# Cutting the last 128 rows into four pieces, and letting each late partial sum enter the result by its own matmul

## The chip, the cores and the metric

One core of a Trainium2 chip. The metric is the device time of one execution in microseconds, as the median of repeated runs. A profile's span, from the first to the last instruction, is some 1.7 us shorter than the time of the same run (667.04 against 668.75 in before). Engines: PE does matmuls, DVE and ACT sum rows, POOL issues the loads, SP the stores.

## The reference

```python
def setup_inputs():
    B, H, W = 4, 4224, 4224
    return {"x": np.random.randn(B, H, W).astype(np.float32)}

def reference(x):
    ps = np.cumsum(np.cumsum(x, axis=1), axis=2)
    diag = np.diagonal(ps, axis1=1, axis2=2)
    return np.cumsum(diag, axis=1).astype(np.float32)
```

All of x (285 MB in fp32) has to be read; what comes out is 4 x 4224 numbers.

## The kernel before

The loads cast to bf16 on the way (the page has 285.47 MB read from HBM, 142.47 MB on the queue). For most of x, matmuls with a selector matrix and row sums on DVE and ACT share the work. The last 384 outputs of the last batch are treated apart, as their rows arrive last: `part_a` is 256 rows, `part_b` the last 128, which come in three pieces of columns (`bcuts`). Each piece is divided among three engines (`shares`): its first `wp` columns go to PE, which folds them into 256 columns of PSUM; the next `wa` go to ACT; the rest to DVE.

```python
# ... after the loads of part_a:
            bcuts = [(2432, TB), (640, 2432), (0, 640)]
            for c0, c1 in bcuts:
                nc.gpsimd.dma_start(out=part_b[:, c0:c1], in_=x[b, TB:N, c0:c1])
# ... fold_a, carry, two scans and the store of the first 3840 outputs ...
        fold_b = psum_s.tile([P, 256], FP32, name="fold")
        fin_a = psum_s.tile([1, 2 * P], FP32, name="fin_a")
        fin_b = psum_s.tile([1, P], FP32, name="fin_b")
        shares = [(768, 512), (768, 512), (0, 320)]
        n = 1
        for i, ((c0, c1), (wp, wa)) in enumerate(zip(bcuts, shares)):
            fold_in(fold_b, part_b, c0, c0 + wp, 256, start=i == 0)          # PE
            act_sum(tsum[:, n : n + 1], part_b[:, c0 + wp : c0 + wp + wa])   # ACT
            if i == 2:
                row_sums(tsum[:, n + 2 : n + 3], fold_b)                     # DVE
            row_sums(tsum[:, n + 1 : n + 2], part_b[:, c0 + wp + wa : c1])   # DVE
            n += 2
            if i == 0:                                                       # PE, fp32
                matmul(fin_b, arows[:, 0:1], weights[:, 2 * P : GW], start=True)
                matmul(fin_b, arows[:, 1:2], weights[:, P : 2 * P])
                matmul(fin_a, arows[:, 0:1], weights[:, 0 : 2 * P], start=True)
                matmul(fin_a[:, P : 2 * P], arows[:, 1:2], weights[:, 0:P])
        ttot = last.tile([P, 1], FP32, name="ttot")
        row_sums(ttot, tsum)
        matmul(fin_b, ttot, weights[:, 0:P])
# ... yl = fin_a + c12, store; yl = fin_b + c12, store
```

`arows` are the row sums of part_a, `ttot` those of part_b. I call the four matmuls on arows "the fins" (the trace shows each fp32 matmul as two passes, so the two on fin_a are a group of x4), and "piece two" is the second of the pieces.

## Time and profile before

| | before |
|---|---|
| time, median of 3 runs (lowest to highest) | 669.03 us (668.8 to 669.93) |
| span of the profiled run | 667.04 us |
| DMA queue, share of 16 engines | 99.7% |
| DVE, PE, ACT busy | 50%, 32%, 21% |
| last landing (slowest engine's part of the last piece) | 663.43 us |
| yl<-fin_b, the last addition, starts | 664.77 us |

How to read it: the time is where the stream of loads ends, plus a tail. The tail has a part that never changes (from the start of yl<-fin_b to the end of the span 2.27 to 2.30 us in every one of the twenty profiles of this study: the addition, the store, the closing semaphores) and a part that the kernel decides. I call that part the **lag**: from the last landing to the start of yl<-fin_b, 1.34 us here. The lines are in the prediction.

### The profile page before, as it was taken

To read this page: it belongs to the slowest core of one execution; us is meant where nothing else is said; L and a number is where in the kernel's file an instruction comes from. 1 tells how busy PE (TensorE), PEld (TensorE's weight loads), DVE (VectorE), ACT (ScalarE), POOL (GpSimd) and SP (SyncE) were. 2 spreads that over 40 slices of the span, in tenths; PEclk is the share of its full clock that TensorE was granted. 3 is DMA by queue.
4 is the path that set the end of the run, shared out by engine and by line. 5 is a ranking of instruction groups with operands and counts; after the bars stand their busy time and mean duration, and the time that the engine had idled before them with its cause. 6 is when DMAs were issued, how large, how long until landed. Compare 5 with 4: busy or idle time off the path is not lost.

```text
span 667.0 us, 2828 instructions
## 1 busy us (share of the span) xinstructions
PE 215.1 (32%) x967; PEld 97.2 (15%) x967; DVE 336.3 (50%) x376; ACT 140.1 (21%) x225; POOL 27.0 (4%) x56
## 2 busy tenths in 40 slices
PE   0071522403118254140321633504032254250426
PEld 0030211101003022010110311201011122120202
DVE  2043617366924351745883415266398241635687
ACT  0001120406300103040630020304063002030436
POOL 5000000000000000000000000000000000001000
PEclk9995857666558586665655957567565586765758
DMA  9999999999999999999999999999999999999997
GB/s 203 219 219 219 218 219 219 217 217 216 208 215 219 219 219 217 216 219 219 219 219 215 216 211 217 220 219 216 216 216 219 220 215 218 216 215 219 216 207 144
DMA packets 7384, 143.25 MB, mean 215 GB/s; under 512 B 669, under 2 KB 842, under 8 KB 1866
## 3 DMA queue, kind: packets, MB, share of 16 engines
q0 software_dynamic: 7008, 142.47, 99.7%
q1 hardware_dynamic: 362, 0.61, 0.3%
q8 instruction: 7, 0.11, 0.1%
q14 instruction: 7, 0.06, 0.0%
HBM read 285.47 MB, written 0.07 MB: 428 GB/s over the span
## 4 chain that ended last, share of the span: by engine, by line
another core or an unknown queue 42%; DVE 25%; PE 23%; DMA 5%; issue 4%; DVEq 0%; POOLq 0%
PE d L198 23%; DVE acc L215 17%; DVE mu L218 7%; DMA strip<-in_x_dram 5%; PE fold L198 1%; DVE pu L215 0%; DVE c L397 0%; DVE c L218 0%; DVE tsum L215 0%; DVE acc L301 0%; DVE acc L304 0%; PE carry_ps L198 0%; DVE rows L331 0%; DVEq L218 0%
## 5 line engine op out<-in xcount | busy, mean ns | idle before, releaser
L218 DVE SCALAR_TENSOR_TENSOR mu<-strip,um 128x768 bf16<-128x768 bf16 (+1 forms) x129 | 110.7, 908 | 314.4 <-DMA strip<-in_x_dram 222.3
L198 PE MATMUL d<-strip,sel 128*11 128x384 bf16 x603 | 140.0, 406 | 344.4 <-DMA strip<-in_x_dram 344.4
L210 ACT ACTIVATE dump<-strip 128x416 bf16<-128x416 bf16 (+8 forms) x112 | 128.4, 1146 | 523.2 <-DMA strip<-in_x_dram 520.2
L215 DVE TENSOR_REDUCE acc<-strip 128x6 f32<-128x4608 bf16 (+6 forms) x23 | 195.9, 8518 | 0.0
L198 PEld LDWEIGHTS <-sel 128*11 128x11 bf16 x849 | 86.1, 101 | 526.3 <-issue 488.4
L198 PE MATMUL d<-mu,sel 128*11 128x384 bf16 x243 | 59.7, 355 | 67.5 <-DVE mu L218 67.4
L75 POOL DMA_DIRECT2D strip<-in_x_dram x24 | 16.5, 687 | 555.5 <-DVE acc L215 414.5
L210 ACT ACTIVATION_READ_ACCUMULATOR dump<-strip 128x1 f32 x112 | 20.9, 186 | 0.0
L218 DVE DVE_READ_ACCUMULATOR mu<-strip,um 128x1 f32 x129 | 10.6, 82 | 0.0
L198 PE MATMUL d<-ident,rows 128*11 128x128 f32 x24 | 5.2, 378 | 16.5 <-DVE rows L340 16.5
L198 PE MATMUL fold<-strip,ident_h 128*128 128x480 bf16 (+1 forms) x14 | 4.3, 458 | 8.4 <-DMA strip<-in_x_dram 8.4
L198 PE MATMUL d<-halves,rows 128*11 128x64 f32 x48 | 5.7, 304 | 0.0
L198 PEld LDWEIGHTS d<-halves,rows 128*11 128x11 f32 x48 | 5.1, 136 | 2.1 <-issue 2.1
L198 PEld LDWEIGHTS d<-ident,rows 128*11 128x11 f32 x24 | 2.6, 118 | 18.2 <-DVE rows L340 11.5
L215 DVE TENSOR_REDUCE pu<-d 11x1 f32<-11x384 f32 x4 | 2.2, 546 | 5.5 <-PE d L198 5.5
L397 DVE TENSOR_TENSOR_SCAN c<-ones_row,carry,c 11x384 f32<-11x384 f32 x4 | 4.0, 1006 | 0.1
L397 DVE TENSOR_TENSOR_SCAN c<-ones_row,carry,d 11x384 f32<-11x384 f32 x4 | 4.0, 1001 | 0.1
L198 PEld LDWEIGHTS <-ident_h 128*128 128x128 bf16 x20 | 2.2, 112 | 12.2 <-issue 11.8
L215 DVE TENSOR_REDUCE parts<-strip 128x3 f32<-128x3072 bf16 x1 | 3.4, 3350 | 0.0
L198 PE MATMUL d<-hmu,sel 128*11 128x384 bf16 (+2 forms) x3 | 0.7, 286 | 6.7 <-DVE hmu L218 6.7
L372 POOL DMA_DIRECT2D strip<-in_x_dram x2 | 1.4, 716 | 29.2 <-DVE acc L215 29.2
L215 DVE TENSOR_REDUCE tsum<-strip 128x1 f32<-128x384 bf16 (+2 forms) x3 | 1.7, 568 | 0.9 <-DMA strip<-in_x_dram 0.9
(78 smaller groups left out, 36.0 us busy)
## 6 DMA issues: line engine op xcount, KB each, us to landing
strip<-in_x_dram POOLq DMA_DIRECT2D x19, 6336.0 KB, 69.6
strip<-in_x_dram POOLq DMA_DIRECT2D x5, 3168.0 KB, 55.3
strip<-in_x_dram POOLq DMA_DIRECT2D x1, 1080.0 KB, 45.3
strip<-in_x_dram POOLq DMA_DIRECT2D x1, 768.0 KB, 48.2
head<-in_x_dram SPq DMA_DIRECT2D x1, 528.0 KB, 3.9
strip<-in_x_dram POOLq DMA_DIRECT2D x1, 448.0 KB, 51.1
strip<-in_x_dram POOLq DMA_DIRECT2D x1, 416.0 KB, 49.5
strip<-in_x_dram POOLq DMA_DIRECT2D x1, 160.0 KB, 51.4
```

The lines of the kernel that those rows point to most:

```text
L75: nc.gpsimd.dma_start(out=o, in_=x[b, r0 : r0 + f * P, :].rearrange("(p f) w -> p f w", f=f))
L198: nc.tensor.matmul(o, lhsT=lhsT, rhs=rhs, start=start, stop=False, skip_group_check=True)
L210: nc.scalar.activation(out=dump[:, :w], in_=src, func=ACT.Copy, accum_out=acc)
L215: nc.vector.reduce_sum(out=acc, in_=src, axis=AX.X)
L218: nc.vector.scalar_tensor_tensor(out=o, in0=i, scalar=1.0, in1=m, op0=ALU.mult, op1=ALU.mult, accum_out=acc,)
L372: nc.gpsimd.dma_start(out=part_a[:, :, c0:c1], in_=src_a[:, :, c0:c1])
L397: nc.vector.tensor_tensor_scan(out=c12[:, i, :], data0=ones_row, data1=src, initial=carry[:, i : i + 1], op0=ALU.mult, op1=ALU.add,)
```

## The change

The intent: make the piece that arrives last small, so that little is left to sum when it lands, and spare the reduction `ttot` at the very end: sums that come late enter fin_b by a matmul of their own. The fold narrows to 128 columns, and yl<-fin_a with its store moves forward.

```diff
-            bcuts = [(2432, TB), (640, 2432), (0, 640)]
+            bcuts = [(2688, TB), (1024, 2688), (384, 1024), (0, 384)]
...
-        shares = [(768, 512), (768, 512), (0, 320)]
+        shares = [(640, 384), (640, 512), (0, 320), (0, 128)]
         for i, ((c0, c1), (wp, wa)) in enumerate(zip(bcuts, shares)):
+            if i < 2:
+                fold_in(fold_b, part_b, c0, c0 + wp, P, start=i == 0)
+                a, v = tsum[:, 2 * i + 1 : 2 * i + 2], tsum[:, 2 * i + 2 : 2 * i + 3]
+            else:
+                a, v = ttot[:, 2 * i - 3 : 2 * i - 2], ttot[:, 2 * i - 2 : 2 * i - 1]
+            act_sum(a, part_b[:, c0 + wp : c0 + wp + wa])
+            row_sums(v, part_b[:, c0 + wp + wa : c1])
             if i == 0:
+                # fin_a's two matmuls, then fin_b's two, on arows
+                nc.vector.tensor_add(
+                    out=yl[:, : 2 * P], in0=fin_a, in1=c12[0:1, 1, : 2 * P]
+                )
+            if i == 1:
+                row_sums(tsum[:, 5:6], fold_b)
+                row_sums(ttot[:, 0:1], tsum[:, 0:6])
+                matmul(fin_b, ttot[:, 0:1], weights[:, 0:P])
-        row_sums(ttot, tsum)
-        matmul(fin_b, ttot, weights[:, 0:P])
+        for k in range(1, 5):
+            matmul(fin_b, ttot[:, k : k + 1], weights[:, 0:P])
...
```

More of the change, by code (lines that the diff above doesn't have):

```diff
@@ L421 @@
         row_sums(arows, asum)
-        fold_b = psum_s.tile([P, 256], FP32, name="fold")
+        fold_b = psum_s.tile([P, P], FP32, name="fold")
         fin_a = psum_s.tile([1, 2 * P], FP32, name="fin_a")
         fin_b = psum_s.tile([1, P], FP32, name="fin_b")
-        shares = [(768, 512), (768, 512), (0, 320)]
-        n = 1
+        yl = last.tile([1, GW], FP32, name="yl")
+        ttot = last.tile([P, 5], FP32, name="ttot")
+        shares = [(640, 384), (640, 512), (0, 320), (0, 128)]
         for i, ((c0, c1), (wp, wa)) in enumerate(zip(bcuts, shares)):
-            fold_in(fold_b, part_b, c0, c0 + wp, 256, start=i == 0)
-            act_sum(tsum[:, n : n + 1], part_b[:, c0 + wp : c0 + wp + wa])
-            if i == 2:
-                row_sums(tsum[:, n + 2 : n + 3], fold_b)
-            row_sums(tsum[:, n + 1 : n + 2], part_b[:, c0 + wp + wa : c1])
-            n += 2
+            if i < 2:
[5 more added lines that the diff above has]
+            row_sums(v, part_b[:, c0 + wp + wa : c1])
@@ L436 @@
             if i == 0:
+                matmul(fin_a, arows[:, 0:1], weights[:, 0 : 2 * P], start=True)
+                matmul(fin_a[:, P : 2 * P], arows[:, 1:2], weights[:, 0:P])
                 matmul(fin_b, arows[:, 0:1], weights[:, 2 * P : GW], start=True)
                 matmul(fin_b, arows[:, 1:2], weights[:, P : 2 * P])
-                matmul(fin_a, arows[:, 0:1], weights[:, 0 : 2 * P], start=True)
-                matmul(fin_a[:, P : 2 * P], arows[:, 1:2], weights[:, 0:P])
-        ttot = last.tile([P, 1], FP32, name="ttot")
@@ L442 @@
-        row_sums(ttot, tsum)
-        matmul(fin_b, ttot, weights[:, 0:P])
-        yl = last.tile([1, GW], FP32, name="yl")
-        for fin, c0, c1 in ((fin_a, 0, 2 * P), (fin_b, 2 * P, GW)):
-            nc.vector.tensor_add(
-                out=yl[:, c0:c1], in0=fin, in1=c12[0:1, 1, c0:c1]
-            )
-            nc.sync.dma_start(
-                out=out[b, T0 + c0 : T0 + c1].unsqueeze(0), in_=yl[:, c0:c1]
-            )
+                nc.vector.tensor_add(
+                    out=yl[:, : 2 * P], in0=fin_a, in1=c12[0:1, 1, : 2 * P]
+                )
@@ new lines @@
+            if i == 1:
[4 more added lines that the diff above has]
+            matmul(fin_b, ttot[:, k : k + 1], weights[:, 0:P])
+        nc.sync.dma_start(
+            out=out[b, T0 : T0 + 2 * P].unsqueeze(0), in_=yl[:, : 2 * P]
+        )
+        nc.vector.tensor_add(
+            out=yl[:, 2 * P :], in0=fin_b, in1=c12[0:1, 1, 2 * P :]
+        )
@@ L455 @@
+        nc.sync.dma_start(out=out[b, T0 + 2 * P : N].unsqueeze(0), in_=yl[:, 2 * P :])
 _INS = ['x']
```

## The prediction

> **What bounds the kernel now.** I read the page top down: engine shares, the 40 slices, then the chain that ended last, and after that the timeline of the last ten microseconds engine by engine. The 40 slices say what sets nearly all of the time:
>
> ```profile
> DMA  9999999999999999999999999999999999999997
> GB/s 203 219 219 219 218 219 219 217 217 216 208 215 219 219 219 217 216 219 219 219 219 215 216 211 217 220 219 216 216 216 219 220 215 218 216 215 219 216 207 144
> ```
>
> Every slice but the last has the DMA engines at 90% or more, and the page's queue section puts 99.7% of 16 engines' span on the software queue, while the busiest compute engine, DVE, is at 50%. The kernel is one stream of loads of about 663 us plus a tail after the last byte. The change moves no byte in or out of that stream: bcuts still cover the same 4096 columns of the last 128 rows. So only the tail can move.
>
> The tail is read from DVE's timeline, because the last stretch of the chain alternates between DVE and PE:
>
> ```profile
> 660.30 0.66 DVE L215 TENSOR_REDUCE asum<-fold_a 128x2 f32<-128x512 f32 x1
> 661.06 0.16 DVE L215 TENSOR_REDUCE arows<-asum 128x2 f32<-128x10 f32 x1
> 661.14 0.54 DVE L215 TENSOR_REDUCE tsum<-strip 128x1 f32<-128x384 bf16 x1
> 662.62 0.69 DVE L215 TENSOR_REDUCE tsum<-strip 128x1 f32<-128x512 bf16 x1 [0.94 <-DMA strip<-in_x_dram]
> 663.22 0.41 DVE L215 TENSOR_REDUCE tsum<-fold 128x1 f32<-128x256 f32 x1
> 663.55 0.47 DVE L215 TENSOR_REDUCE tsum<-strip 128x1 f32<-128x320 bf16 x1
> 664.13 0.16 DVE L215 TENSOR_REDUCE ttot<-tsum 128x1 f32<-128x8 f32 x1
> 664.21 0.40 DVE L446 TENSOR_TENSOR yl<-fin_a,c 1x256 f32<-1x256 f32 x1
> 664.77 0.28 DVE L446 TENSOR_TENSOR yl<-fin_b,c 1x128 f32<-1x128 f32 x1 [0.16 <-PE fin_b L198]
> ```
>
> ```profile
> 661.37 0.60 PE L198 MATMUL fin_b<-weights,arows 128*1 128x128 f32 x4 [0.39 <-DVE arows L215]
> 661.80 0.81 PE L198 MATMUL fin_a<-weights,arows 128*1 128x256 f32 x4
> 662.64 0.49 PE L198 MATMUL fold<-strip,ident_h 128*128 128x256 bf16 x3
> 664.35 0.38 PE L198 MATMUL fin_b<-weights,ttot 128*1 128x128 f32 x2 [1.22 <-DVE ttot L215]
> ```
>
> To be seen: DVE has one real wait, 0.94 us for the second piece of the last rows; from 662.62 it runs without a gap until ttot. The landings in the trace (last of a load's semaphore counts) are 660.44, 662.60 and 663.43 us for the three pieces. ACT's sum of the third piece starts at 663.51 and its accumulator read ends at 664.08; DVE's ends at 664.02. So after the last byte (663.43) come: sum 0.65 us, ttot at 664.13 (0.16), one matmul in two passes at 664.35 (0.38), yl at 664.77 (0.28), the output's issue at 665.07, its landing at 666.13, closing semaphores until 667.04. Some 3.6 us in all, of which the change can touch the first 1.3 us: 0.2% of the time.
>
> [...] In the trace DVE does run in program order: yl<-fin_a, ready since the 662.62 at which fin_a ended, stands until 664.21 behind everything written before it. [...] 320, 384 and 512 columns take 474, 543 and 686 ns, 1.1 ns per column. [...] The trace: the 16 counts of the last piece come from 661.24 to 663.43. [...]
>
> **The change, part by part.**
>
> Landings. On the slowest of the 16 engines a row of 1280 bytes took 97 ns from start to start, one of 3584 bytes some 265: proportional to bytes plus about 3 ns. Pieces of 1408, 1664, 640 and 384 columns are 8 rows each on that engine. Scaling the old landings, they come at about 660.14, 662.13, 662.91 and 663.47. The last byte is 0.04 us later (8 more rows at 3 ns, one more semaphore write). The one more load costs POOL 0.55 us near 612, 50 us before its data, hidden.
>
> What it removes from the end: the wait of ttot for both sums. ACT's part of the last piece falls from 320 to 128 columns: 0.47 to 0.31 us (0.83 ns per column, from 512 and 320), DVE's from 320 to 256: 0.47 to 0.41. The reduction ttot (0.16 and some 0.1 for its wait) leaves the end. The fold of piece two halves: 414 to 281 ns (estimate, 1.04 ns per column less).
>
> What it adds: four matmuls of two passes, each pass 0.108 us after the last (the four fin_b passes of before start at that spacing), so 0.22 us each.
>
> What it moves, and this decides: the order of instructions on DVE is now: first piece's sum, yl<-fin_a, second piece's sum, fold, ttot, third piece's sum, fourth's, yl<-fin_b. Worked through, with starts 0.08 us or so ahead of the previous end where nothing is waited for:
> - arows is where it was, 661.06 to 661.22, as nothing ahead of it depends on the new cuts. PE starts fin_a (now first) at 661.37: starts at 0, 0.215, 0.43, 0.54, last end 662.18. fin_b's passes follow until PE is free at 662.45[...].
> - DVE: yl<-fin_a can't start before 662.22 (0.04 after PE, as at 664.77 before) and holds DVE for 0.33. Piece two has been there since 662.13, so it now waits behind yl: start 662.55 in place of 662.17.
> - sum of 512 columns holds 0.60: fold at 663.15, ends 663.43; ttot with a wait of 0.10 at 663.53; third piece's sum at 663.61, ends 664.08; fourth's at 664.01, ends 664.42.
> - ACT: second piece done at 662.92, third at 663.57, fourth at 664.07: never last.
> - PE: total's matmul at 663.74, ACT's of piece three behind it; DVE's of piece three at 664.13; then ACT's of piece four at 664.35; DVE's of piece four could start at 664.47 but PE is free at 664.56: two passes, end 664.94.
> - yl<-fin_b at 664.98, against 664.77 before: 0.2 us later. The output's issue, landing and closing follow at the same distance; the first output leaves two microseconds earlier, which nothing waits for.
>
> Sum: gains of 0.06 to 0.16 (smaller sums) and 0.26 (ttot), taken back because DVE is not free when the last piece lands (664.01 against 663.47). Net +0.2 us: 669.03 + 0.2 = 669.2.
>
> **Rivals.** (1) The intended one: the end hangs on the last landing. Then from 663.47: 0.08 start, 0.41 sum, 0.06, two matmuls 0.60, yl at about 664.66, 0.1 us faster: 668.9. For it: DVE did wait 0.94 us for piece two before, so there is slack in its queue; against it: fin_a on PE ends at 662.18, after piece two has landed, so yl<-fin_a uses up that slack. (2) The stream decides: the extra piece, smaller rows, or another spread of the 16 engines move the last landing. For it: the engines finish 2.2 us apart, so one slow engine is what counts, and the three runs of before lie 1.1 us apart with nothing changed. Against: bytes per engine are the same[...]. 0 to +0.3 us beyond mine, or noise of either sign. (3) PE becomes the bound because its granted clock drops to half in the tail: the passes would double and add some 0.5 us, 669.7. Before, it was full from 658 to past 665, and the change adds PE work; unlikely.
>
> **Range and chances.** All three rivals lie within 0.7 us, 0.1% of the time. The spread of runs (668.8 to 669.93) is wider than the effect, so the range is mostly that spread: 668.6 to 669.9. A change of 2% would be 13 us, more than everything after the last byte; 0.01 for each side is left for the unforeseen, 0.98 for within 2%.
>
> **What would show it right or wrong.** Right: in DVE's timeline yl<-fin_a runs for about 0.4 us at 662.2 and the second piece's sum begins directly after it, not with a wait for a DMA; there is no wait between it and the last piece's sum, which begins 0.5 us after its landing; ttot's last matmul waits for DVE or PE, not ACT; yl<-fin_b stands later after the last landing than the 1.34 us of before (mine: 1.5). Wrong: a DMA wait ahead of the last sum on DVE, yl<-fin_b within 1.25 us of the last landing (rival 1), or a last landing more than 0.2 us from its old place (rival 2).

Piece two's five folds: their spacing was not measured in before, where folds of 256 columns start 108 ns apart. The sum has DVE reach the fold at 663.15, behind piece two's sum, and took the folds as done by then, the author's estimate; it comes to yl<-fin_b at 664.98, 0.2 us later than before, and so to 669.2. The 1.04 ns per column in the estimate for the fold is the slope of DVE's long sums in before: 5.55 us for 5184 columns, 11.35 for 10752.

## The result, and the profile after

| | before | after |
|---|---|---|
| time, median of 6 runs (lowest to highest) | 669.29 (668.8 to 669.93) | 669.97 (668.85 to 670.82) |
| span of the profiled run | 667.04 | 667.99 |
| last landing | 663.43 | 663.38 |
| start of yl<-fin_b | 664.77 | 665.70 |
| lag | 1.34 | 2.32 |

All kernels gave correct results. The ratio is 1.001, interval 0.9997 to 1.0022. The predicted 669.2 missed by 0.8 us, and 669.97 lies above the stated 668.6 to 669.9. The profiled run itself took 669.70 us.

The stream is much what it was (of the page's DMA digits only the last differs; the GB/s differ by 8 at most in a slice before the last):

```profile
DMA  9999999999999999999999999999999999999996
GB/s 202 219 219 219 218 219 217 219 219 219 216 211 214 214 220 219 219 219 217 214 219 218 219 219 219 216 212 216 216 219 219 218 215 214 219 218 219 219 204 132
```

The timeline of DVE in the changed kernel (start, duration, engine, line, operation, what it waited for):

```profile
660.57 0.16 DVE L215 TENSOR_REDUCE arows<-asum 128x2 f32<-128x10 f32 x1
...
662.35 0.41 DVE L443 TENSOR_TENSOR yl<-fin_a,c 1x256 f32<-1x256 f32 x1 [1.16 <-PE fin_a L198]
662.69 0.66 DVE L215 TENSOR_REDUCE tsum<-strip 128x1 f32<-128x512 bf16 x1
663.80 0.29 DVE L215 TENSOR_REDUCE tsum<-fold 128x1 f32<-128x128 f32 x1 [0.44 <-PE fold L198]
...
665.70 0.28 DVE L455 TENSOR_TENSOR yl<-fin_b,c 1x128 f32<-1x128 f32 x1 [0.63 <-PE fin_b L198]
```

And PE's:

```profile
660.88 1.44 PE L198 MATMUL fin_a<-weights,arows 128*1 128x256 f32 x4
662.11 1.06 PE L198 MATMUL fin_b<-weights,arows 128*1 128x128 f32 x4
663.10 0.66 PE L198 MATMUL fold<-strip,ident_h 128*128 128x128 bf16 x5
664.41 1.25 PE L198 MATMUL fin_b<-weights,ttot 128*1 128x128 f32 x10 [0.65 <-DVE ttot L215]
```

The order is the predicted one (yl<-fin_a, then piece two's sum directly behind it). What is not predicted: the fins take 2.29 us where 1.25 was reckoned, so piece two's folds end at 663.76 and not before the 663.15 at which the sum has DVE reach them, and DVE waits. The durations double as PE's granted clock halves (1.00 to 0.50; a pass takes 0.213 us in place of 0.108). The view by stretches shows it; its columns are the stretch, its length, busy us of PE, PEld, DVE, ACT and POOL with instruction counts, then the granted clock (the share of its full clock that PE was given), the DMA share and GB/s. First the kernel before, then the changed one:

```profile
657.00:660.50 3.50, 1.48 (x10) 0.56 (x9) 3.01 (x7) 2.27 (x6) 0.00 (x0) 1.00 1.07 211
660.50:663.50 3.00, 2.21 (x14) 1.08 (x13) 1.96 (x5) 1.44 (x4) 0.00 (x0) 1.00 0.45 83
```

```profile
657.00:660.50 3.50, 1.44 (x12) 0.94 (x12) 2.97 (x6) 2.31 (x7) 0.00 (x0) 0.95 1.09 212
660.50:663.50 3.00, 2.89 (x16) 1.28 (x14) 1.63 (x4) 1.77 (x6) 0.00 (x0) 0.50 0.53 90
```

Granted clock 1.00 against 0.50 from 660.5 to 663.5. The trace's clock records give the edges: before, full from 655.60 to 665.84 (10.24 us); after, full from 653.34 to 660.16 (6.82 us), half to 663.58 (3.42 us), full again.

### The profile page after: what moved, and what is told of

It reads as the page before. It is cut to its first block, busy times and chain, and to the rows that moved or that the text cites. A ratio compares the mean times of both kernels' runs of the same rounds, so it can differ in the third digit from the quotient of the medians.

```text
span 668.0 us, 2857 instructions
## 1 busy us (share of the span) xinstructions
PE 214.5 (32%) x979; PEld 97.8 (15%) x979; DVE 336.6 (50%) x377; ACT 140.4 (21%) x227; POOL 27.5 (4%) x57
## 4 chain that ended last, share of the span: by engine, by line
another core or an unknown queue 38%; DVE 24%; PE 22%; DMA 12%; issue 4%; DVEq 0%; POOL 0%; POOLq 0%
PE d L198 21%; DVE acc L215 16%; DMA strip<-in_x_dram 12%; DVE mu L218 6%; PE fin_b L198 0%; DVE pu L215 0%; DVE c L218 0%; PE fin_a L198 0%; PE fold L198 0%; DVE acc L304 0%; DVE acc L301 0%; PE fold_a L198 0%; POOL strip L372 0%; PE carry_ps L198 0%
## 5 line engine op out<-in xcount | busy, mean ns | idle before, releaser
L210 ACT ACTIVATE dump<-strip 128x416 bf16<-128x416 bf16 (+9 forms) x113 | 128.6, 1138 | 522.7 <-DMA strip<-in_x_dram 519.9
L198 PE MATMUL d<-mu,sel 128*11 128x384 bf16 x243 | 58.3, 346 | 67.5 <-DVE mu L218 67.3
L75 POOL DMA_DIRECT2D strip<-in_x_dram x24 | 16.5, 688 | 556.0 <-DVE acc L215 416.9
L198 PE MATMUL fold<-strip,ident_h 128*128 128x128 bf16 (+1 forms) x18 | 4.7, 432 | 9.2 <-DMA strip<-in_x_dram 9.2
L372 POOL DMA_DIRECT2D strip<-in_x_dram x2 | 1.4, 714 | 27.6 <-DVE acc L215 27.6
L375 POOL DMA_DIRECT2D strip<-in_x_dram x4 | 2.2, 550 | 7.9 <-DMA strip<-in_x_dram 7.9
```

The source lines that it names most:

```text
L75: nc.gpsimd.dma_start(out=o, in_=x[b, r0 : r0 + f * P, :].rearrange("(p f) w -> p f w", f=f))
L198: nc.tensor.matmul(o, lhsT=lhsT, rhs=rhs, start=start, stop=False, skip_group_check=True)
L210: nc.scalar.activation(out=dump[:, :w], in_=src, func=ACT.Copy, accum_out=acc)
L372: nc.gpsimd.dma_start(out=part_a[:, :, c0:c1], in_=src_a[:, :, c0:c1])
```

## The experiments

**Theory (clock):** the difference in lag is the clock's, which depends on when the clock happens to turn in a run, not on the change. **Rivals:** (order) the new order on DVE costs it, at any clock; (joins) the five matmuls at the end cost it.

One table for all profiles; the times are medians of the runs with that kernel. "On" is when the clock turned full at the end of the stream, "tail" the granted clock from 660.5 to 663.5, "lead" the time from the start of arows to the last landing.

| run | on | tail | lead | last landing | lag | time (runs) |
|---|---|---|---|---|---|---|
| before | 655.60 | full | 2.37 | 663.43 | 1.34 | 669.29 (6) |
| before_again | 653.67 | half | 2.79 | 663.53 | 2.27 | 669.79 (1) |
| after | 653.34 | half | 2.81 | 663.38 | 2.32 | 669.97 (6) |
| after_again | 652.92 | full | 2.81 | 663.75 | 1.26 | 669.00 (5) |
| after_third | 656.25 | full | 2.41 | 664.13 | 1.55 | 669.77 (6) |
| before_warm | 652.54 | full | 2.65 | 663.44 | 1.34 | 670.26 (5) |
| before_warm_b | 652.70 | full | 2.64 | 663.49 | 1.34 | 669.37 (6) |
| before_warm2 | 653.33 | full | 2.78 | 664.49 | 1.34 | 669.82 (6) |
| after_warm | 654.17 | full | 2.67 | 663.75 | 1.30 | 668.83 (5) |
| after_warm_b | 657.06 | full | 2.26 | 664.96 | 1.70 | 670.45 (6) |
| after_warm2 | 655.57 | full | 2.39 | 664.79 | 1.58 | 670.48 (6) |
| cuts_only | 653.60 | half | 2.81 | 663.41 | 2.22 | 670.26 (5) |
| joins_only | 652.79 | full | 2.78 | 663.49 | 1.39 | 669.43 (6) |
| yl_late | 653.86 | half | 2.81 | 663.65 | 2.37 | 670.02 (1) |
| after_fins2 | 653.87 | half | 2.80 | 663.63 | 3.61 | 671.54 (1) |
| no_fold2 | 653.57 | half | 2.84 | 663.58 | 1.43 | 668.99 (5) |
| no_fold2_b | 653.31 | half | 2.80 | 663.56 | 1.43 | 669.46 (5) |
| no_fold2_warm | 655.39 | full | 2.41 | 663.56 | 1.42 | 668.88 (5) |
| seven_joins | 654.94 | full | 2.81 | 663.65 | 1.42 | 669.11 (5) |
| seven_joins_warm | 653.80 | full | 2.68 | 663.44 | 1.43 | 669.12 (5) |

### Both kernels once more: after_again, before_again, after_third

No edit.

> The changed kernel once more, unaltered. Theory (clock): in the first profile the granted clock was 0.5 from 660.2 to 663.6 us, so the ten matmul passes ahead of piece two's folds took twice as long, the fold came to DVE at 663.80 in place of my 663.15, and yl<-fin_b stood 2.32 us after the last landing. [...]this profile either shows the clock full through 660 to 664 and yl<-fin_b at about 1.5 to 1.6 us after the last landing, or half there and again 2.2 to 2.4. Ratio over five rounds 1.0005 to 1.0015. Rival (order on DVE alone): 2.2 to 2.4 whatever the clock.

> The kernel before once more, unaltered, for a second sample of the clock's phase. Clock theory: full clock from 660 to 664 again gives yl<-fin_b 1.3 to 1.4 us after the last landing; half clock there gives 1.9 to 2.5, since ten passes stand ahead of the second fold here too. Rival (the old order is immune): 1.3 to 1.4 whatever the clock.

> The changed kernel unaltered, for another profile and five more times. Lag 1.25 to 1.6 us if the clock is full from 660 to 664, 2.2 to 2.4 if half; span less 2.27 us less the lag is the last landing, which in the profiles so far lay anywhere from 663.4 to 664.8. Ratio to before within 0.0015 of 1, with either sign.

Ratios: after_again 0.9998 (0.9985 to 1.001), so the expected 1.0005 to 1.0015 was missed; after_third 1.0009 (0.9993 to 1.0025). The kernel before, at half clock; DVE, PE, and the stretch:

```profile
662.72 0.69 DVE L215 TENSOR_REDUCE tsum<-strip 128x1 f32<-128x512 bf16 x1 [1.36 <-DMA strip<-in_x_dram]
664.24 0.42 DVE L215 TENSOR_REDUCE tsum<-fold 128x1 f32<-128x256 f32 x1 [0.84 <-PE fold L198]
...
665.80 0.28 DVE L446 TENSOR_TENSOR yl<-fin_b,c 1x128 f32<-1x128 f32 x1 [0.15 <-PE fin_b L198]
```

```profile
663.54 0.67 PE L198 MATMUL fold<-strip,ident_h 128*128 128x256 bf16 x3
```

```profile
660.50:663.50 3.00, 2.92 (x11) 1.10 (x10) 1.44 (x4) 1.48 (x5) 0.00 (x0) 0.50 0.46 85
```

The old kernel has the same wait for PE's fold (0.84 us) and loses 0.93 us of lag (2.27 against 1.34): the clock hits it as it hits the changed one, and the changed kernel at full clock has 1.26. So the 1 us between the first two profiles is not the change's. That shows only that lag and clock go together; the interventions below test the direction.

after_third has full clock but a late turn-on (656.25) and an arows that is late against the stream (lead 2.41), as in the very first profile of before. This is the case the prediction was worked out for:

```profile
661.72 0.16 DVE L215 TENSOR_REDUCE arows<-asum 128x2 f32<-128x10 f32 x1
...
662.87 0.41 DVE L443 TENSOR_TENSOR yl<-fin_a,c 1x256 f32<-1x256 f32 x1 [0.53 <-PE fin_a L198]
663.21 0.66 DVE L215 TENSOR_REDUCE tsum<-strip 128x1 f32<-128x512 bf16 x1
663.81 0.27 DVE L215 TENSOR_REDUCE tsum<-fold 128x1 f32<-128x128 f32 x1
...
665.68 0.28 DVE L455 TENSOR_TENSOR yl<-fin_b,c 1x128 f32<-1x128 f32 x1 [0.62 <-PE fin_b L198]
```

From the start of arows: yl<-fin_a after 1.15 (predicted 1.16), piece two's sum 1.49 (1.49), fold 2.09 (2.09), yl<-fin_b 3.97 (3.92). Piece two landed at 662.79, and its sum stands behind yl<-fin_a until 663.21. Lag 1.55, predicted 1.51.

### Holding the clock full: before_warm, after_warm, and again as _b

The edit, in both kernels; dummy matmuls into a bank nobody reads, in places where PE waits (three ahead of the carry, one behind it, three behind the second fold_a):

```diff
+            def keep_warm(n):
+                for _ in range(n):
+                    matmul(warm, ident_h, wide_of[0][:, :512], start=True)
...
+            keep_warm(3)
         carry_ps = psum_s.tile([NG, 2], FP32, name="carry_ps")
...
+            keep_warm(1)
         carry = smalls.tile([NG, 2], FP32, name="carry")
...
         fold_in(fold_a, part_a, c0, cp, 256)
+        keep_warm(3)
```

> The kernel before with the same seven dummy matmuls. Clock theory: lag of yl<-fin_b 1.3 to 1.4 us, time at the lower end of before's runs, 668.5 to 669.0, and 0.1 to 0.3 us under after_warm: with the clock equal, my +0.2 for the change is left. Rival (only the changed kernel is touched by the clock): no gain over before, ratio 1.000 within 0.0005.

> The changed kernel with seven dummy matmuls of 512 columns in PE's idle time of the last rows (three before the carry, one after it, three after the second fold_a), so that [...]the clock stays full. Clock theory: no 0.5 between 657 and 664, folds of piece two done by 663.1, yl<-fin_b 1.45 to 1.65 us after the last landing, 668.9 to 669.4 us, 0.5 to 0.9 faster than the changed kernel of the same rounds. Rival (DVE's order or the five last matmuls cost the time): lag stays at 2.2 or more, and the time with the changed kernel's.

> The kernel before with the seven dummies, again. Clock theory: this profile has full clock from 660 to 664 and lag 1.3 to 1.4; slow runs, if any, are late streams. If the profile falls on half clock in the tail in spite of the dummies, they don't hold it, and after_warm's five fast runs were luck.

> The changed kernel with the seven dummies, again. Clock theory: full clock in the tail, lag 1.25 to 1.6, span between 667.0 and 668.7 by where the stream ends. Luck: a run at half clock with lag 2.2 or more.

Ratios to before: before_warm 1.0006 (0.9992 to 1.002), after_warm 0.9989 (0.9977 to 1.0002), before_warm_b 0.9998 (0.9984 to 1.0013), after_warm_b 1.0009 (0.9994 to 1.0024). All four profiles have full clock in the tail, and lags of 1.30 to 1.70 only. With the dummies of the later runs it is eight of eight, against five of twelve without. The sharpest pairs have nearly the same turn-on: without dummies, all seven runs in which the clock turned on between 653.31 and 653.87 fell back to half at 660; with them, before_warm2 (653.33) and seven_joins_warm (653.80) did not.

The times are another matter, and here the expectation failed: before_warm had three of five runs at 670.3 to 670.5, and after_warm_b five of six above 670. The one profile among those, after_warm_b, has full clock and a lag of 1.70, but its **stream** ended at 664.96, 1.5 us later than in the first profile. Its third load landed at 97.6 us against 95.3 in before, long ahead of the first dummy, so the dummies didn't cause that delay. The same holds for all four late streams (after_third, before_warm2, after_warm_b, after_warm2): the 25th load, which landed at 649.58 in before, was already 0.67, 1.07, 1.55 and 1.39 us late, and no dummy runs before 655. The stream's end is a second draw, made before the tail begins. What the unprofiled slow runs of before_warm had, I can't say.

### More dummies: before_warm2, after_warm2

Ten in place of seven, two of them ahead of the last matmuls of d.

> The kernel before with ten dummy matmuls of 512 columns: two ahead of the last part of d, two before the carry, two after it, four after the second fold_a. [...] Clock theory: all five runs in the fast group (under 669.2), none near 670. In the first try with seven dummies three of five were at 670.3 and I saw no profile of those; if the five split again, the dummies do something else than keep the clock, and this theory needs another support. Rival (two groups from something other than the clock): about half of the runs at 669.6 to 670.1.

> The changed kernel with the same ten dummies. Clock theory: all five runs under 669.2, mean within 0.2 us of before_warm2; the changed kernel's slower average is then its slow group alone. Rival (the change costs time at any clock): 0.2 to 0.5 us over before_warm2.

Ratios 1.0002 (0.999 to 1.0013) and 1.0011 (0.9999 to 1.0024). Both profiles: full clock, lag 1.34 and 1.58, but streams that ended at 664.49 and 664.79. The expected "all under 669.2" failed for the times. As a test of the time it is inconclusive; as a test of the clock it adds two profiles at full clock. before_warm2 is useful otherwise: its stream is 1.06 us later than before's, and the lag is the same 1.34.

### One half of the change at a time: cuts_only, joins_only

cuts_only has the new pieces and shares with the old joining; joins_only the old pieces with the new joining:

```diff
 # cuts_only, against the changed kernel
-            if i < 2: ... else: ...    (own columns of ttot, own matmuls)
+            if i == 1:
+                row_sums(tsum[:, n : n + 1], fold_b)
+                n += 1
+        row_sums(ttot, tsum)
+        matmul(fin_b, ttot, weights[:, 0:P])
 # joins_only, against the changed kernel
+            bcuts = [(2432, TB), (640, 2432), (0, 640)]
+        shares = [(768, 512), (768, 512), (0, 320)]
+        for k in range(1, 3):
```

> The four pieces and their shares, with the old joining: one ttot over all sums, one matmul, fin_b ahead of fin_a, both yl at the end. Runs in two groups by the clock. Full clock: DVE is free when the last piece lands (no yl in its queue), sum 0.41, ttot 0.26, matmul 0.38: yl<-fin_b about 1.2 us after the last landing, 668.7 to 668.9. Half clock: the second fold is late as in the others, 1.9 to 2.3 us after landing, 669.5 to 670.0. If the joining is what costs in the slow group, this one's slow group lies 0.2 to 0.4 us under the changed kernel's 670.15.

> The old three pieces with the new joining: fin_a first and yl<-fin_a early, ttot over what is there by the second piece, the third piece's two sums by their own matmuls. Full clock: yl<-fin_a is hidden in DVE's wait for piece two (landing at 662.6), so DVE's third sum ends at 664.0 as before, two matmuls more: 1.2 to 1.35 us after the last landing, 668.7 to 668.9. Half clock: three matmuls of two passes at the end, if at half clock 0.43 each: 2.2 to 2.7, 669.8 to 670.3. If the cuts are what costs, this is as before.

Ratios 1.0008 (0.9996 to 1.002) and 0.9998 (0.9986 to 1.001). cuts_only's profile fell on half clock: lag 2.22, 0.1 us under the changed kernel's 2.32 at half clock, not the 0.2 to 0.4 of the rival. Its five runs (669.62 to 670.61) are no faster than the changed kernel's slow ones. joins_only at full clock: 1.39, 0.05 us over before and just over the expected 1.2 to 1.35. ttot is no longer behind DVE's last sum but ahead of it, so that this sum starts 0.40 us after the landing (663.89) where it was 0.12 in before (663.55); the saved ttot makes up for most of that. So neither half carries the 1 us: against before at the same clock, cuts_only has 0.05 us less lag (2.22 against 2.27) and joins_only 0.05 us more. Each was seen at one clock only, and the times can't resolve such differences.

### Undoing the moved addition: yl_late

```diff
             if i == 0:
-                nc.vector.tensor_add(
-                    out=yl[:, : 2 * P], in0=fin_a, in1=c12[0:1, 1, : 2 * P]
-                )
...
         for k in range(1, 5):
             matmul(fin_b, ttot[:, k : k + 1], weights[:, 0:P])
+        nc.vector.tensor_add(
+            out=yl[:, : 2 * P], in0=fin_a, in1=c12[0:1, 1, : 2 * P]
+        )
```

> The changed kernel with yl<-fin_a moved behind the last sum on DVE, as it was before the change: one part undone. My prediction had it as the cause of +0.2 us. From the profiles since: with arows 2.8 us before the last landing, as in most, the lag stays at 1.2 to 1.3 at full clock (the yl was hidden in the wait for piece two), and 2.2 to 2.3 at half clock (the fold's wait covers it). If the step of the prediction holds, the lag falls to 1.1 or less at full clock.

Half clock. DVE:

```profile
662.37 0.69 DVE L215 TENSOR_REDUCE tsum<-strip 128x1 f32<-128x512 bf16 x1 [0.90 <-DMA strip<-in_x_dram]
664.12 0.29 DVE L215 TENSOR_REDUCE tsum<-fold 128x1 f32<-128x128 f32 x1 [1.07 <-PE fold L198]
```

Piece two's sum now starts at once when its data lands (662.34), and it helps nothing: DVE then waits 1.07 us for the fold. Lag 2.37 against 2.32. At half clock the order on DVE is not the cause; at full clock this run doesn't say.

### Doubling the suspected cost: after_fins2

```diff
+                dup = psum_s.tile([1, 2 * P], FP32, name="dup")
+                matmul(dup, arows[:, 0:1], weights[:, 0 : 2 * P], start=True)
+                matmul(dup[:, P : 2 * P], arows[:, 1:2], weights[:, 0:P])
+                matmul(dup[:, 0:P], arows[:, 0:1], weights[:, 2 * P : GW])
+                matmul(dup[:, 0:P], arows[:, 1:2], weights[:, P : 2 * P])
```

> The changed kernel with the ten passes of arows issued a second time, into a bank nobody reads, between the fins and piece two's folds: the suspected cost doubled. Theory: at full clock the folds end 1.08 us later (10 units of 0.108), DVE's fold waits for them, and the lag goes from 1.26 to 1.30 to about 2.1 to 2.3, like half clock without the copy; if this run falls on half clock, 4.0 to 4.5. Rival (what costs at half clock is the matmuls at the end, after the landing): the lag stays within 0.3 of the kernel's without the copy.

DVE and PE:

```profile
662.96 0.66 DVE L215 TENSOR_REDUCE tsum<-strip 128x1 f32<-128x512 bf16 x1
665.34 0.29 DVE L215 TENSOR_REDUCE tsum<-fold 128x1 f32<-128x128 f32 x1 [1.72 <-PE fold L198]
```

```profile
663.22 1.70 PE L198 MATMUL dup<-weights,arows 128*1 128x256 f32 x8
```

The eight copies took PE from 663.22 to 664.85, when the folds could start; the lag went from 2.32 to 3.61. It is less than the 4.0 to 4.5 expected for half clock because the clock came back at 664.11, in the middle of the copies. PE's time between arows and piece two's folds passes into the lag one for one: from the start of the fins to the fold on DVE it is 2.92 us in the changed kernel (660.88 to 663.80) and 4.20 here (661.14 to 665.34), 1.28 more, and the lag is 1.29 more.

### Taking the dependence away: no_fold2, no_fold2_b, no_fold2_warm

Piece two loses its fold; ACT takes 768 of its columns, DVE 896. The fold of piece one is summed early, yl<-fin_a goes last:

```diff
-        shares = [(640, 384), (640, 512), (0, 320), (0, 128)]
+        shares = [(640, 384), (0, 768), (0, 320), (0, 128)]
+            if i == 0:
+                fold_in(fold_b, part_b, c0, c0 + wp, P, start=True)
             if i < 2:
-                fold_in(fold_b, part_b, c0, c0 + wp, P, start=i == 0)
...
             if i == 0:
+                row_sums(tsum[:, 5:6], fold_b)
...
             if i == 1:
-                row_sums(tsum[:, 5:6], fold_b)
```

> A repair of the changed kernel: piece two has no fold on PE (ACT takes 768 of its columns, DVE 896), so nothing on DVE waits for PE between the fins and the end, and yl<-fin_a goes to the end of DVE's queue. Theory (the tail's length hangs on PE's clock through the second fold): yl<-fin_b 1.1 to 1.3 us after the last landing, both at full clock and with 0.5 between 660 and 664, where the kernels with the fold had 2.2 to 2.3. Time: end of the stream plus that, so 668.6 to 669.7 with the stream's own spread of up to 1.4 us, mean 0.3 to 0.6 under before of the same rounds. Rival (DVE's load is what counts): DVE has 0.2 us more to do here, so the lag is 0.2 longer than the changed kernel's of the same clock.

> The repair again. Its first profile was at half clock with lag 1.43, where the fold kernels have 2.2 to 2.4. Full clock: 1.1 to 1.25, since the first of the last five matmuls waits for ttot alone. Half clock: 1.4 to 1.5. Mean time 0.1 to 0.5 us under before of the same rounds.

> The repair with the seven dummies. Lag 1.1 to 1.25 at full clock; spread of the times that of the stream's end alone, 668.5 to 670. If the dummies cost anything[...], lag is 1.3 or more.

Ratios 0.9995 (0.9983 to 1.0007), 0.9998 (0.9984 to 1.0012), and with dummies 0.9989 (0.9976 to 1.0001). The first, at half clock: DVE, PE and the stretch:

```profile
662.27 1.09 DVE L215 TENSOR_REDUCE tsum<-strip 128x1 f32<-128x896 bf16 x1 [0.70 <-DMA strip<-in_x_dram]
663.46 0.16 DVE L215 TENSOR_REDUCE ttot<-tsum 128x1 f32<-128x6 f32 x1
663.53 0.80 DVE L215 TENSOR_REDUCE ttot<-strip 128x1 f32<-128x320 bf16 x2
...
665.01 0.28 DVE L456 TENSOR_TENSOR yl<-fin_b,c 1x128 f32<-1x128 f32 x1 [0.36 <-PE fin_b L198]
```

```profile
661.05 1.44 PE L198 MATMUL fin_a<-weights,arows 128*1 128x256 f32 x4 [0.16 <-DVE arows L215]
662.28 1.06 PE L198 MATMUL fin_b<-weights,arows 128*1 128x128 f32 x4
663.67 1.30 PE L198 MATMUL fin_b<-weights,ttot 128*1 128x128 f32 x10 [0.33 <-DVE ttot L215]
```

```profile
660.50:663.50 3.00, 2.68 (x12) 0.99 (x10) 2.09 (x6) 1.81 (x6) 0.00 (x0) 0.50 0.60 102
```

The fins are as slow as in the changed kernel (1.44 and 1.06 us, clock 0.50), but DVE no longer waits for PE: lag 1.43 at half clock, twice, and 1.42 at full. The four half-clock profiles with piece two's fold and one set of fins have 2.22 to 2.37. This settles the link: half clock costs by way of piece two's fold, which is what stands behind the slow fins on PE and ahead of the last sums on DVE. The rival (DVE's load) is out: it asked for 0.2 us more lag than the changed kernel's. The expected 1.1 to 1.3 was not reached, nor the 1.1 to 1.25 with dummies: in the first of them, with five join matmuls starting at 663.67 and 0.22 us apart, PE is done at 664.97, 0.6 us after DVE's last sum (664.33).

### Taking ttot out of the joins' way: seven_joins, seven_joins_warm

Against no_fold2, cut; ttot's own matmul moves up too, and piece two's two sums get columns of ttot:

```diff
-        ttot = last.tile([P, 5], FP32, name="ttot")
+        ttot = last.tile([P, 7], FP32, name="ttot")
...
             if i == 0:
-                row_sums(tsum[:, 5:6], fold_b)
+                row_sums(tsum[:, 3:4], fold_b)
+                row_sums(ttot[:, 0:1], tsum[:, 0:4])
...
-        for k in range(1, 5):
+        for k in (1, 2, 3, 4, 6, 5):
             matmul(fin_b, ttot[:, k : k + 1], weights[:, 0:P])
```

> The repair with ttot over piece one alone, so that its matmul is done by 662 at full clock, and piece two's two sums joining by their own matmuls too: seven in all, the last piece's ACT sum last. If the queue of joins behind ttot set the repair's 1.42, the lag is now set by the last sum on ACT (0.72 us after the landing, in the repair's traces) plus 0.05, one matmul 0.38 and 0.04: 1.2 to 1.25, at half clock up to 663.6 as well, if no more than one of the joins is still queued. If it stays at 1.4, the queue was not the cause. Time 0.2 us under the repair's at the same end of the stream.

> The same with the seven dummies: full clock in the tail, lag 1.2 to 1.25; time 668.5 to 668.7 when the stream ends at 663.5, later by as much as the stream is.

Missed: 1.42 and 1.43 again; ratios 0.9999 (0.9985 to 1.0013) and 0.9995 (0.9982 to 1.0007). PE's joins in the first:

```profile
663.41 1.63 PE L198 MATMUL fin_b<-weights,ttot 128*1 128x128 f32 x12 [0.79 <-ACT dump L210]
```

Inside this group two joins run at 663.41; the third starts only at 664.00, when ACT's sum of piece three is read out (663.95), and with the three behind it in the queue it is one run of 0.22 us each to 665.03. ttot had only handed its place to another late sum. So, by this reading of the lines, it would need fewer joins at the end and not an earlier ttot; no run tests that. No version is shown to beat both kernels: the lowest ratio is 0.9989, of after_warm and of no_fold2_warm; both intervals touch 1, and after_warm repeated gave 1.0009.

## Why the prediction was wrong, point by point

**What bounds the kernel.** Right. The stream takes all but the tail, and the ratio is within 0.1%.

**The landings.** Predicted 663.47 for the last one. Of the fourteen profiles of kernels with four pieces, eleven have 663.38 to 663.75, the other three 664.13 to 664.96: the change's part is small, as predicted, but the stream's own spread I hadn't reckoned with. before_warm2, with the old three pieces, has 664.49.

**The order on DVE.** Right in mechanism and, at the same clock and a like turn-on, in size. After after_third's arows everything stands within 0.05 us of the prediction. The five profiles of the changed kernel at full clock (with and without dummies) show what the step amounts to: lead plus lag is 3.97 in four of them and, for the longest lead, 4.07. The chain from arows to yl<-fin_b takes 3.97 us, and only with a lead over some 2.7 us (an estimate, 3.97 less the 1.26 of that one profile) does the last landing set the end. The old kernel has 1.34 at leads from 2.37 to 2.78: landing-bound in all four full-clock profiles. So at full clock the change costs 0.21 us (1.55 against 1.34) where arows is late and gains 0.08 where it is early. This rests on the order and times of the lines; no run undoes the order at full clock. I took one trace's lead, 2.37, for the kernel's; it is the shortest of those of before. The lead goes with the clock's turn-on: 2.26 to 2.41 in the five profiles where it came after 655, 2.64 to 2.84 in the fifteen where it came earlier; the matmuls ahead of arows run at half clock until then, which is the likely reason; no run tests it.

**The step that failed.** It is the cost of PE's passes, and with it rival 3: "its granted clock drops to half in the tail ... some 0.5 us, 669.7. Before, it was full from 658 to past 665, and the change adds PE work; unlikely." The passes in my sum took 0.108 us. In the changed kernel's first profile the clock was half, and they took 0.213: piece two's folds ended at 663.76 and not before 663.15 (at full clock, in after_third, the five took 0.45 us), DVE waited 0.44 us for them where my sum has no wait, and the lag was 2.32 where 1.51 was reckoned. Nor is it unlikely: seven of the twelve profiles without dummies had half clock, one of before's two among them. And its size was set too low, 0.5 us, where the lag grew by 0.93 in before (1.34 to 2.27) and by 0.8 to 1.1 in the changed kernel (1.26 to 1.55, to 2.32). Doubling the fins' 1.08 us passes whole into the lag as long as piece two's fold is queued behind them.

This doesn't account for the whole miss. The profiled run with half clock took 669.70 us, inside my range. That this is also rival 3's figure is luck: its lag was 2.32 and not some 2.0, and my base of 669.03 was a median 0.28 us above the profiled run of before (668.75). The three runs above the range (670.24, 670.36 and 670.82) were not profiled, and half clock with a stream that ends as in that profile doesn't reach them. A late stream, as in other profiles, would; whether they had one stays open.

**The range.** "The range is mostly that spread", 668.8 to 669.93, from three runs, was too narrow. Over all rounds the unchanged kernel had 57 runs from 668.62 to 671.18, with 28% above my upper end of 669.9. So a median of six runs of the changed kernel just above it is no sign of the change.

**What the change did.** Pooled, the changed kernel's 17 runs average 669.84 with a standard error of 0.21, before's 57 runs 669.53 with 0.09. The difference of 0.3 us is under 1.4 standard errors: not resolved. Nor do the dummies show in the times: with them, 17 runs each, before averages 669.65 (standard error 0.17) and the changed kernel 669.91 (0.24). They shortened the lag in the profiles; the times don't show it under the stream's spread. Why there is no gain from the change is read from the profiles: a smaller last piece pays only if someone is free when it lands, and in four of the changed kernel's five full-clock profiles DVE's chain from arows ends last instead (in the repaired kernels, PE's queue of joins).

**Open.** Why streams end up to 1.5 us late (in the two latest, after_warm_b and after_warm2, the third load already landed some 2.2 us late); and what the unprofiled runs above 670 had, those of the changed kernel and of before_warm.

## What to carry to other kernels

Split a tail into the part that waits for the last byte and the part that waits for an earlier chain, and take the slack between the two from several profiles, not from one; shrinking the last piece helps only where that slack is positive. Where the last microseconds hold fp32 matmuls ahead of something that DVE waits for, reckon with both granted clocks (1.00 and 0.50 here) and, better, keep PE out of the path between the last landings and the last sums. With effects below 0.1%, the measure is the lag in the traces; the times carry two draws, each of about a microsecond.
